# Seven block products for the output projection of a hybrid decoder step, with operand and weight sums woven in

## The chip, the cores and the metric

One Trainium2 chip, one core of it. The metric is the device time of one execution in microseconds, median of the runs. Engines: TensorE (PE for the matmuls, PEld for the loads of its stationary operand), VectorE (DVE), ScalarE (ACT), GpSimd (POOL) and SyncE (SP). Transfers are issued from two queues: SP's (`DMA`) and ACT's (`WDMA`, weights only).

## The reference

One layer of a decoder with three groups of heads (6 mLSTM "A", 6 gated DeltaNet "B", 4 HGRN2 "C", 128 wide each). 1024 prompt tokens, 16 meta tokens and 8 x 8 sample tokens pass through it, in float32:

```
h = rmsnorm(x) * norm_w
aq, ak, av, ao, ..., z = split(h @ w_in)          # w_in 2048 x 8984
hcat = concat(mlstm(...), gated_deltanet(...), hgrn2(...))   # 16 heads, chunked scans with state
y = headnorm(hcat) * out_norm_w * silu(z)         # tokens x 2048
x + y @ w_out                                     # w_out 2048 x 2048
y_prompt, y_sample = rmsnorm(x + y @ w_out) * final_norm_w
```

Besides the two y outputs the new states of all heads are returned. The change concerns the product `y @ w_out` for the 1024 prompt tokens.

## The kernel before, in words

The prompt is worked on in two halves of 512 tokens (`Half`); the first half carries the 64 sample tokens and the meta tokens as well. For each half, the input projection runs head by head in the order `ORDER` (C0 B0 A0 B1 A1 C1 B2 A2 B3 A3 C2 B4 A4 B5 A5 C3), and the heads' scans are interleaved with the matmuls of later heads. Then comes the output product for both halves.

Matmul precision: every float32 operand is split into a rounded part (hi) and a rest (lo), both in the fp32r type, and a product is hi·hi + hi·lo + lo·hi: three matmuls (two for the samples, whose hi and lo stand side by side as 128 columns).

Weights come as *pieces*: 128 x 512 float32 tiles in the order of the list `pieces`. `feed_raw` issues a piece's load on ACT's queue into one of 5 `wraw` buffers; `feed_split` makes `whi` (a cast on ACT) and `wlo` (a subtraction on DVE); `feed_ahead` keeps splits up to three pieces and loads up to seven pieces ahead of the piece in use. `o_raw` loads pieces of `w_out`.

Order of work: matmuls are written out in a fixed order. Everything else is a generator (`Stream`) in one of the queues of `Weave` (scan, fin, post, bg). A planner clock (`Clock`) adds up estimated costs per engine. After every matmul group, `pump` runs the next segment of each queue whose due time on TensorE's clock has come. A generator sets when its next segment is due by `ck.last`. `drain` moves the planner's clock on until a stream is done. Loads may be moved ahead by the scheduling framework as soon as their buffer is free, except those marked `keep_in_program_order`.

- `prep_B` (queue bg) prepares the second half's normalized input during the first half, through three `px` buffers, into DRAM (`hb_dram`).
- `gdn_scan` is a DeltaNet head: products on TensorE, coefficients sent through DRAM to give `Bb`, 15 steps of substitution on DVE (`substitute`), then doubling of the blocks (`pz`, `pyy`), then the chain over chunks (`pr`, `pw`, `pu2`, `po2`).
- `finish` (queue fin) normalizes a head's output, transposes it through DRAM, multiplies by `zs`, splits it into hi (ACT) and lo (POOL) and stores both parts in `y_dram`.

The output product before: for the first half and then the second, for each group `cg` of 512 output columns, 5 (or 4) token tiles accumulate over 16 heads `k` in PSUM banks `oacc`. At the end of a group, x is loaded, added on DVE, squared on ACT and multiplied by `final_norm_w` on POOL; `final_norm` scales and stores. The two last units have two token tiles each, so that little is left behind the last matmul. `load_y` brings the first half's y into the buffers of the projection's input, and the second half's y during the first half's last group.

Of the kernel before, what the change touches and what calls it, by code (L numbers as in the profile page):

```python
# [6 lines left out]
F32 = mybir.dt.float32  # L7
# [179 lines left out]
OUT_UNITS = ([(cg, range(5)) for cg in range(4)], [(cg, range(4)) for cg in range(3)] + [(3, range(2)), (3, range(2, 4))])  # L187
# [3 lines left out]
def hybrid_step(ctx, tc, i, o):  # L191
# [27 lines left out]
    def bank(name):  # L219
        return ps.tile([P, 512], F32, tag="ps", name=name)  # L220
# [22 lines left out]
    def o_raw(k, cg):  # L243
        raw = wp.tile([P, 512], F32, tag="wraw", name="wraw", bufs=5)
        WDMA(raw, i["w_out"][0, P * k:P * (k + 1), 512 * cg:512 * (cg + 1)])
        return raw

# [95 lines left out]
    for units in OUT_UNITS:  # L343
        for cg, _ in units:
            for k in range(NK):
                pieces.append((o_raw, k, cg))
# [256 lines left out]
    y_dram = [dp.tile([NH, P, w], F32R, name=f"y{w}") for w in (2 * NSAMP + 2 * HALF, 2 * HALF)]  # L603
# [233 lines left out]

    def finish(half, head, outs, ssq, scale, zs):
# [30 lines left out]
        yield  # L869
        yhi, ylo = zs.bitcast(F32R), y.bitcast(F32R)  # L870
# [4 lines left out]
        d = y_dram[half.index][head].bitcast(F32)  # L875
        for part, t in enumerate((yhi, ylo)):
            t = t.bitcast(F32)
            at_ = 2 * NSAMP if half.first else 0
            DMA(d[:, at_ + HALF * part:at_ + HALF * (part + 1)], t[:, 0:HALF])
            if half.first:  # L880
                DMA(d[:, NSAMP * part:NSAMP * (part + 1)], t[:, HALF:WS])
# [90 lines left out]
    def mlstm_scan(half, h, kT, qT, vT, tho, zs, nm, em, st):  # L972
# [118 lines left out]
        weave.add("fin", finish(half, h, hxs, ssq, 0.25, zs))  # L1091
# [60 lines left out]
    def gdn_scan(half, h, ck_, cq, cv, zs, Gb, eG, bb, st):  # L1152
# [65 lines left out]
        ready = ck.t["T"] + 7.0  # L1218
# [99 lines left out]
        ck.last += 8.0  # L1318
# [76 lines left out]
        weave.add("fin", finish(half, HA + h, hxs, ssq, 1.0, zs))  # L1395
# [22 lines left out]
    def hgrn_scan(half, h, kT, lf, qT, vT, zs, st):  # L1418
# [152 lines left out]
        weave.add("fin", finish(half, HA + HB + h, hxs, ssq, 0.25, zs))  # L1571
# [91 lines left out]
    def load_y(half, g):  # L1663
        w = y_dram[half.index].shape[-1]
        yT[half.index][g] = [hp.tile([P, 2, w], F32R, tag=f"h{g}{part}", name=f"y{g}{part}") for part in (0, 1)]
        for q in range(4):
            DMA(yT[half.index][g][q // 2][:, q % 2].bitcast(F32), y_dram[half.index][4 * g + q].bitcast(F32))

    def y_block(half, k, n, part):

        at_ = HALF * part + P * n
        return yT[half.index][k // 4][k % 4 // 2][:, k % 2, at_:at_ + P]

    hB, yT = {}, [{}, {}]
    for half, groups in zip(halves, group_lists):
        if not half.first:
            weave.drain_queue("bg")
            hT = hB
        seen = set()
        for n, group in enumerate(groups):  # L1680
            fresh = []
            for name, _, _ in group:
                if name not in seen:
                    seen.add(name)
                    fresh.append(name)
            if half.first and n == 6:
                weave.add("bg", prep_B())
            after = None
            if n == len(groups) - 1:
                if half.first:  # L1690
                    weave.drain_queue("bg")
                    after = load_hB
                else:
                    after = lambda g: load_y(halves[0], g)
# [12 lines left out]

    ys_flat = o["y_sample"].rearrange("b t d -> (b t) d")
    tags = ["a", "b", "c", "d", "e", "f", "g", "h", "j", "a", "b", "c", "d", "e", "f", "g", "h", "j", "k", "u"]

    def final_norm(toks, some, res, ss, fr, late):
        for n in some:
            cnt = toks[n][1]
            V.tensor_reduce(fr[:cnt, n:n + 1], ss[:cnt, n], op=ALU.add, axis=AX.X)
            V.tensor_scalar(fr[:cnt, 8 + n:9 + n], fr[:cnt, n:n + 1], 1.0 / D, EPS, op0=ALU.mult, op1=ALU.add)
            G.tensor_tensor(fr[:cnt, 16 + n:17 + n], fr[:cnt, 8 + n:9 + n], halfneg[:cnt, 0:1], op=ALU.pow)
        yield
        for n in some:
            _, cnt, _, dst = toks[n]
            for cg in range(4):  # L1720
                t, r = res[n, cg], fr[:cnt, 16 + n:17 + n]
                if cg == 3 and late:
                    V.scalar_tensor_tensor(t[:cnt], t[:cnt], r, fnw[cg][:cnt], op0=ALU.mult, op1=ALU.mult)
                elif cg == 3 or late and cg == 2:
# [4 lines left out]
                yield  # L1729

# [12 lines left out]
    fnw = []  # L1743
    for half in halves:
        toks = []
        for n, (c0, cnt) in enumerate(half.tiles):
            if half.first and n == 0:
                toks.append((0, NSAMP, xs_flat, ys_flat))
            else:
                a = HALF * half.index + c0  # L1750
                toks.append((c0, P, i["x_prompt"][0, a:a + P], o["y_prompt"][0, a:a + P]))
        nt = len(toks)
        ss = sp.tile([P, 8, 4], F32, tag="oss", name="oss")
        fr = sp.tile([P, 24], F32, tag="fr", name="fr")
        res = {}
        for cg, some in OUT_UNITS[half.index]:
            ccols = slice(512 * cg, 512 * (cg + 1))
            accs = {n: bank("oacc") for n in some}
            for k in range(NK):
                whi, wlo = next_piece()  # L1760
                for n in some:
                    yh, yl = (y_block(half, k, n, part) for part in (0, 1))
                    both = toks[n][1] == NSAMP
                    T.matmul(accs[n], yh, whi, start=k == 0, stop=False)
                    T.matmul(accs[n], yh, wlo, start=False, stop=both and k == NK - 1)
                    if not both:
                        T.matmul(accs[n], yl, whi, start=False, stop=k == NK - 1)
                    if n == some[0]:
                        feed_ahead()
                    weave.pump()  # L1770
                if half.first and cg == 3 and k % 4 == 3:
                    if k == 3:
                        weave.drain_queue("scan")
                        weave.drain_queue("fin")
                    load_y(halves[1], k // 4)
            if half.first and cg == 0:
                weave.drain_queue("scan")
                weave.drain_queue("fin")
                fnw = [sp.tile([P, 512], F32, tag=f"s{t}", name="fnw", bufs=1) for t in ("7", "8", "9", "B")]
                for t, c in zip(fnw, range(4)):  # L1780
                    DMA(t, i["final_norm_w"][512 * c:512 * (c + 1)].rearrange("(x d) -> x d", x=1).partition_broadcast(P))
                weave.add("bg", norm_states())
            weave.drain_queue("post")
            late = not half.first and cg == 3 and some[-1] == nt - 1
            for n in some:
                _, cnt, xsrc, _ = toks[n]
                t = row(tags[(nt * cg + n) % len(tags)], "res")[:, 0:512]
                DMA(t[:cnt], xsrc[:, ccols])
                ck.begin()
                V.tensor_tensor(t[:cnt], t[:cnt], accs[n][:cnt], op=ALU.add)  # L1790
                scr = sp.tile([P, 512], F32, tag="px", name="oscr", bufs=3)
                if cnt == NSAMP:
                    S.copy(scr[:cnt], accs[n][cnt:2 * cnt])
                    V.tensor_tensor(t[:cnt], t[:cnt], scr[:cnt], op=ALU.add)
                S.activation(scr[:cnt], t[:cnt], AF.Square, accum_out=ss[:cnt, n, cg:cg + 1])
                if not late:
                    G.tensor_tensor(t[:cnt], t[:cnt], fnw[cg][:cnt], op=ALU.mult)
                res[n, cg] = t
            if cg == 3:
                weave.add("post", final_norm(toks, some, res, ss, fr, late))  # L1800
# [35 lines left out]
```

## Time and profile before

| | |
|---|---|
| median of 3 runs | 2501.23 us (2497.94 to 2503.61) |
| the profiled execution | 2499.9 us, of which the span is 2498.2 us |
| mean granted TensorE clock | 0.991 |
| projections | to about 2097 us |
| output product | 2097.2 to 2487.5 us |
| behind the last matmul | 10.7 us |
| moved by DMA | 350.81 MB, 140 GB/s on average |

Busy times are per engine, in us. Matmul records overlap, as matmuls are pipelined, so a matmul's price is taken from the distance between starts. Nearly all instructions carry line L137, that of the recording helper, so groups are told apart by the names of their tiles: `oacc<-whi,y` is a matmul of the output product, `wlo<-wraw,whi` the split of a piece of weights, `res<-res,oacc` the sum out of PSUM.

### The profile page before, as it was taken

What the parts mean: (1) busy time and instruction counts of PE and PEld (TensorE: products, weight loads), DVE (VectorE), ACT (ScalarE), POOL (GpSimd) and SP (SyncE); (2) the same over time, 40 slices, a digit from 0 to 9 for tenths busy, and PEclk for the clock granted to TensorE, in tenths of its full rate; (3) what the DMA queues carried; (4) which work ended last, traced back from release to release, by engine and by line L of the source; (5) the groups of instructions that cost most, each with busy time, mean ns of one, the idle gap of its engine ahead of it and who ended that gap; (6) DMA issues with size and microseconds to landing.
All of it is one profiled execution on the core that took longest, in us unless ns stands there. A gap on an engine that the chain in (4) does not pass through costs nothing.

```text
span 2498.2 us, 43685 instructions
## 1 busy us (share of the span) xinstructions
PE 2437.1 (98%) x16032; PEld 2181.1 (87%) x16032; DVE 1441.9 (58%) x3080; ACT 993.4 (40%) x2428; POOL 548.7 (22%) x743
## 2 busy tenths in 40 slices
PE   6999999999999999999999999999999999999998
PEld 5999999999999999998787888888888888888886
DVE  7765766766647656556854556554654646333435
ACT  5643444443435334343642343343533334222324
POOL 5331211421204212113320113110310102111201
PEclk9999999999999999999999999999999999999999
DMA  6445756766645445348445445454544559526735
GB/s 138 111 119 144 175 131 135 187 147 159 147 108 142 99 119 146 93 112 244 112 121 123 112 120 135 118 134 98 144 118 112 132 124 307 135 84 201 252 100 181
DMA packets 681043, 350.81 MB, mean 140 GB/s; under 512 B 260004, under 2 KB 622076, under 8 KB 680828
## 3 DMA queue, kind: packets, MB, share of 16 engines
q10 hardware_dynamic: 318528, 185.64, 29.4%
q1 hardware_dynamic: 362300, 162.37, 24.9%
q8 instruction: 126, 2.06, 0.3%
q14 instruction: 89, 0.73, 0.1%
HBM read 285.71 MB, written 62.19 MB: 139 GB/s over the span
## 4 chain that ended last, share of the span: by engine, by line
PE 77%; DVE 8%; DMA 6%; issue 3%; ACT 2%; POOL 2%; SPq 1%; ACTq 0%; DVEq 0%; POOLq 0%
PE acc L137 53%; PE oacc L137 13%; DVE wlo L137 2%; DMA wraw<-in_w_in_dram 2%; PE pa L137 1%; PE po L137 1%; SPq L1209 1%; PE pyy L137 1%; PE nd L137 1%; DMA Bb<-db 1%; ACT whi L137 1%; PE pu L137 1%; PE pz L137 1%; DVE Yc L137 1%; DVE Yt L137 1%
## 5 line engine op out<-in xcount | busy, mean ns | idle before, releaser
L137 DVE TENSOR_TENSOR wlo<-wraw,whi 128x512 fp32r<-128x512 f32 x720 | 540.2, 752 | 552.5 <-ACT whi L137 534.7
L137 PE MATMUL acc<-hA,whi 128*128 128x288 f32 (+1 forms) x4544 | 819.6, 302 | 5.3 <-DVE whi L137 5.1
L137 ACT CAST whi<-wraw 128x512 fp32r<-128x512 f32 x720 | 443.9, 618 | 934.9 <-PE acc L137 427.5
L137 PE MATMUL acc<-hB,whi 128*128 128x512 f32 x2272 | 725.3, 401 | 3.6 <-DMA hB<-hblo 3.1
L137 PEld LDWEIGHTS acc<-hA,whi 128*128 128x128 f32 x4544 | 676.1, 190 | 10.2 <-issue 6.5
L137 PE MATMUL acc<-hA,wlo 128*128 128x288 f32 x2240 | 488.5, 298 | 4.7 <-DVE wlo L137 4.7
L137 PEld LDWEIGHTS acc<-hB,whi 128*128 128x128 f32 x2272 | 415.4, 190 | 85.6 <-DMA hB<-hblo 3.9
L137 PE MATMUL acc<-hB,wlo 128*128 128x512 f32 x1120 | 441.6, 394 | 1.5 <-DVE wlo L137 1.5
L137 PEld LDWEIGHTS acc<-hA,wlo 128*128 128x128 f32 x2240 | 365.7, 189 | 6.3 <-DVE wlo L137 6.3
L137 PE MATMUL oacc<-whi,y 128*128 128x512 f32 x1088 | 343.2, 390 | 0.0
L137 PEld LDWEIGHTS acc<-hB,wlo 128*128 128x128 f32 x1120 | 212.1, 189 | 49.4 <-DVE wlo L137 3.4
L137 PEld LDWEIGHTS oacc<-whi,y 128*128 128x128 f32 x1088 | 204.3, 188 | 42.8 <-ACT whi L137 0.8
L137 PE MATMUL oacc<-wlo,y 128*128 128x512 f32 x576 | 224.6, 390 | 2.0 <-DVE wlo L137 2.0
L137 PEld LDWEIGHTS oacc<-wlo,y 128*128 128x128 f32 x576 | 108.2, 188 | 25.4 <-DVE wlo L137 3.3
L137 POOL TENSOR_TENSOR res<-res,fnw 128x512 f32<-128x512 f32 (+1 forms) x34 | 48.6, 1460 | 258.5 <-ACT oscr L137 258.5
L137 POOL TENSOR_TENSOR y<-y,zs 128x592 fp32r<-128x592 f32 (+1 forms) x32 | 46.1, 1441 | 153.2 <-ACT zs L137 138.9
L137 POOL TENSOR_TENSOR qd<-qT,emb 128x512 f32<-128x512 f32 x12 | 16.9, 1404 | 219.1 <-PE po L137 219.0
L137 DVE TENSOR_TENSOR Yt<-Yc,Bb 128x60 f32<-128x60 f32 (+8 forms) x180 | 36.5, 203 | 47.5 <-DMA Bb<-db 42.4
L137 POOL TENSOR_TENSOR hr<-hr,halfneg 128x4 f32<-128x4 f32 (+1 forms) x48 | 44.7, 931 | 70.3 <-DVE hr L137 69.3
L137 POOL TENSOR_TENSOR nrm<-nrm,halfneg 128x10 f32<-128x10 f32 x12 | 24.0, 1998 | 125.0 <-DVE nrm L137 125.0
L137 POOL TENSOR_TENSOR X<-Ex,hk 128x256 f32<-128x256 f32 (+1 forms) x40 | 39.7, 992 | 52.4 <-PE pa L137 40.7
L137 DVE TENSOR_TENSOR Sx<-Sx,lf 128x256 f32<-128x256 f32 (+2 forms) x60 | 35.3, 590 | 20.8 <-ACT Ex L137 18.9
(416 smaller groups left out, 2748.4 us busy)
## 6 DMA issues: line engine op xcount, KB each, us to landing
wraw<-in_w_in_dram ACTq DMA_DIRECT2D x564, 256.0 KB
wraw<-in_w_out_dram ACTq DMA_DIRECT2D x144, 256.0 KB
y<-y SPq DMA_DIRECT2D x16, 576.0 KB
px<-in_x_prompt_dram SPq DMA_DIRECT2D x32, 256.0 KB
yd<-y SPq DMA_DIRECT2D x128, 64.0 KB
out_dram<-sst SPq DMA_DIRECT2D x16, 512.0 KB
s<-yd SPq DMA_DIRECT2D x32, 256.0 KB
y<-zs SPq DMA_DIRECT2D x32, 256.0 KB
```

Of the source, the lines that this page charges most:

```text
L137: return f(out, *a, **k)
L1209: DMA(db[j], Ball[SUB * j:SUB * (j + 1), 0:C, SUB * j:SUB * (j + 1)])
```

## The change: seven products

Let A be y as a 2 x 2 block matrix: rows are the first and second 512 prompt tokens, columns the first eight heads of `ORDER` (`K1`) and the last eight (`K2`). B is `w_out`, its rows cut by the same heads, its columns into two halves of 1024 (column groups j and j + 2, j = 0, 1). The eight block products become seven:

- T1 = B12 - B11, T3 = B22 - B12, T2 = B22 - T1, T4 = B21 - T2
- S1 = A21 + A22, S2 = S1 - A11, S3 = A11 - A21, S4 = A12 - S2
- phase 1: A11·B11, phase 2: A12·B21, phase 3: S2·T2, phase 4: S4·B22, phase 5: S1·T1, phase 6: S3·T3, phase 7: A22·T4; the results are sums of these.

What is done where:

- **Weights' sums.** `combine_weights`, in a new queue "mix", starts when `prep_B` is done and is drained in the middle of phase 1. In 16 rounds it loads four 128 x 512 tiles of `w_out` on SP's queue (held in program order), makes T1 to T4 in place on POOL, and stores them in DRAM (`w_comb`); `c_raw` later loads them as pieces.
- **A's sums.** The second half's `finish` no longer splits: it stores y once, in `y_whole`. During a phase, `fill` makes the next phase's left operand, head by head, in 16 steps and 4 more of the phase after: loads from `y_whole` (held in order, three buffers each, issued two steps ahead), sums on DVE and POOL, and three steps behind the sum a cast on ACT and a subtraction on DVE into the buffers `yT`.
- **Samples** are multiplied in phases 1 to 4 with the same pieces; in phase 3 they need pieces of their own (`other`), so 32 pieces are used there for 16.
- **Results.** x is loaded and added on POOL during the phases (`x_rows`, `x_added`); at the end of each of the two groups of a phase, DVE adds the four banks to one or two of the running sums. The last units are one of four tiles and two of two tiles, of 8 heads each.
- **DeltaNet.** `ready` is 10 after the loads of `Bb` are issued where it was 7, and the pause between the substitution and the doubling is 11 where it was 8 (planner's us).

The diff, cut to its core:

```diff
-        self.queues = {"scan": [], "fin": [], "post": [], "bg": []}
+        self.queues = {"scan": [], "fin": [], "post": [], "bg": [], "mix": []}
...
+HEADS = [{"A": 0, "B": HA, "C": HA + HB}[name[0]] + int(name[1]) for name in ORDER[1:]]
+K1, K2 = HEADS[:NH // 2], HEADS[NH // 2:]
+LAST_UNITS = [(0, range(4)), (1, range(2)), (1, range(2, 4))]
...
+    def c_raw(name, j, kk):
+        raw = wp.tile([P, 512], F32, tag="wraw", name="wraw", bufs=5)
+        WDMA(raw, w_comb[name][NK // 2 * j + kk])
+        return raw
...
+        if not half.first:
+            DMA(y_whole[head], y[:, 0:HALF])
+            return
         yhi, ylo = zs.bitcast(F32R), y.bitcast(F32R)
...
-        ready = ck.t["T"] + 7.0
+        ready = ck.t["T"] + 10.0
...
         yield from substitute()
-        ck.last += 8.0
+        ck.last += 11.0
...
+    def combine_weights():
+        while not prep_stream.done:
+            yield
+        for j in range(2):
+            for kk in range(NK // 2):
+                b11, b12, b21 = (sp.tile([P, 512], F32, tag="px", name="px", bufs=3) for _ in range(3))
+                b22 = sp.tile([P, 512], F32, tag="pxs", name="pxs", bufs=1)
+                for t, heads, cg in ((b11, K1, j), (b12, K1, j + 2), (b22, K2, j + 2), (b21, K2, j)):
+                    tc.keep_in_program_order(DMA(t, i["w_out"][0, P * heads[kk]:P * (heads[kk] + 1), 512 * cg:512 * (cg + 1)]))
+                for dst, a, b in ((b11, b12, b11), (b12, b22, b12), (b22, b22, b11), (b21, b21, b22)):
+                    ck.last = ck.t["T"] + 7.0
+                    yield
+                    G.tensor_tensor(dst, a, b, op=ALU.subtract)
+                ck.last = ck.t["T"] + 20.0
+                yield
+                for n, t in (("T1", b11), ("T3", b12), ("T2", b22), ("T4", b21)):
+                    DMA(w_comb[n][NK // 2 * j + kk], t)
+                    ck.last = ck.t["T"] + 3.0
+                    yield
+                ck.last = ck.t["T"] + 12.0
+                yield
...
+    def phase(u, j, accs, tiles, own=None, other=None, each=()):
+        for kk in range(NK // 2):
+            whi, wlo = next_piece()
+            for n in tiles:
+                yh, yl = (y_block(u, kk, n, part) for part in (0, 1))
+                T.matmul(accs[n], yh, whi, start=kk == 0, stop=False)
+                T.matmul(accs[n], yh, wlo, start=False, stop=False)
+                T.matmul(accs[n], yl, whi, start=False, stop=kk == NK // 2 - 1)
...
+            for g in filling:
+                next(g, None)
+            for f in each:
+                f(NK // 2 * j + kk)
...
+    def fill(at_, u, loads, ops, again=None):
+        for kk in range(NK // 2 + 2):
+            if kk < NK // 2:
+                for x, heads in enumerate(loads):
+                    weave.drain(fins[1, heads[kk]])
+                    tc.keep_in_program_order(DMA(beside[x][(at_ + kk) % 3], y_whole[heads[kk]]))
+                if again:
+                    DMA(yT[u][kk // 2][:, kk % 2, 2 * NSAMP:].bitcast(F32), y_dram[again[kk], :, 2 * NSAMP:].bitcast(F32))
+            if 0 < kk < NK // 2 + 1:
...
+                for e, a, b, op in ops:
+                    e.tensor_tensor(srcs[0], srcs[a], srcs[b], op=op)
+                    ck.sync()
+            yield
+            if kk > 1:
+                hi, lo = parts(u, kk - 2)
+                src = beside[0][(at_ + kk - 2) % 3]
+                ck.begin()
+                S.copy(hi, src)
+                ck.sync()
+                V.tensor_tensor(lo, src, hi, op=ALU.subtract)
+            yield
...
+    fill_with(0, [K1, K2], [(V, 0, ("hi", 0), LESS), (V, 0, ("lo", 0), LESS), (G, 0, 1, PLUS)])
+    for j in range(2):
+        accs, sacc = banks(), bank("oacc")
+        phase(1, j, accs, halfn, own=(sacc, samples(1)), each=[x_rows(1, 0, t1)])
+        ck.begin()
+        for n in halfn:
+            V.tensor_tensor(res[n + 1, j], res[n + 1, j], accs[n], op=ALU.add)
+            squared(n + 1, j)
+        sample_add(j, sacc)
...
+    fill_with(1, [], [(G, ("hi", 1), ("lo", 1), PLUS), (G, 0, ("hi", 0), LESS), (G, 0, ("lo", 0), LESS)])
+    for j in range(2):
+        accs, sacc = banks(), bank("oacc")
+        phase(0, j, accs, halfn, other=(sacc, samples(0)))
+        ck.begin()
+        for n in halfn:
+            V.tensor_tensor(t1[j, n], t1[j, n], accs[n], op=ALU.add)
+        sample_add(j + 2, sacc)
...
+    fill_with(0, [K1, K2], [(G, 0, 1, PLUS)])
...
+    fill_with(1, [K1], [(V, ("hi", 1), 0, LESS), (G, 0, ("lo", 1), PLUS)], again=K1)
...
+    fill_with(0, [K2], [])
```

More of the change, by code (lines that the diff above doesn't have):

```diff
@@ L1090, in mlstm_scan @@
         G.tensor_copy(Cn, last)
-        weave.add("fin", finish(half, h, hxs, ssq, 0.25, zs))
+        add_finish(half, h, hxs, ssq, 0.25, zs)
         if not half.first:
@@ L1729, in final_norm @@
                 yield
+            free.extend(res.pop((n, cg)) for cg in order)
     def norm_states():
@@ L1741, in norm_states @@
         yield
[L1743 to L1788, printed above, removed]
-                ck.begin()
[L1790 to L1800, printed above, removed]
@@ new lines, in x_load, with squared, sample_add @@
+    def x_load(n, cg):
+        t = free.pop(0)
+        cnt, src, _ = toks[n]
+        DMA(t[:cnt], src[:, 512 * cg:512 * (cg + 1)])
+        return t
+    def squared(n, cg, late=False):
+        cnt = toks[n][0]
+        t = res[n, cg]
+        S.activation(oscr[:cnt], t[:cnt], AF.Square, accum_out=ss[:cnt, n, cg:cg + 1])
+        if not late:
+            G.tensor_tensor(t[:cnt], t[:cnt], fnw[cg % 2][:cnt], op=ALU.mult)
+    def sample_add(cg, acc, first=False):
+        t = res[0, cg][:NSAMP]
+        ck.begin()
+        if first:
+            V.tensor_copy(t, acc[:NSAMP])
+        else:
+            V.tensor_tensor(t, t, acc[:NSAMP], op=ALU.add)
+        S.copy(oscr[:NSAMP], acc[NSAMP:2 * NSAMP])
+        V.tensor_tensor(t, t, oscr[:NSAMP], op=ALU.add)
@@ new lines, in fill_with, with x_rows, f, x_added @@
+    def fill_with(*a, **kw):
+        filling.append(fill(NK // 2 * len(filling), *a, **kw))
+    def x_rows(n0, cg0, sums):
+        def f(step):
+            j, x = step // 8, step % 8
+            if 1 <= x < 5:
+                res[x - 1 + n0, j + cg0] = x_load(x - 1 + n0, j + cg0)
+            if 3 <= x < 7:
+                t = res[x - 3 + n0, j + cg0]
+                G.tensor_tensor(t, t, sums[j, x - 3], op=ALU.add)
+        return f
+    def x_added(dst, j, n0, cg0, start):
+        pend = []
+        def f(step):
+            if step > start + 1 and pend:
+                t, x = pend.pop(0)
+                G.tensor_tensor(t, t, x, op=ALU.add)
+                free.append(x)
+            n = step - start
+            if n in halfn:
+                pend.append((dst[j, n], x_load(n + n0, j + cg0)))
+        return f
@@ new lines, in hybrid_step @@
+    weave.add("post", sample_done(2, 3))
+    weave.add("post", final_norm([0], range(4)))
+    fill_with(1, [K1], [(V, ("hi", 1), 0, LESS), (G, 0, ("lo", 1), PLUS)], again=K1)
+    for j in range(2):
+        accs = banks()
+        phase(0, j, accs, halfn, each=[at_step(5, lambda: free.extend(beside[1])), x_added(q, 0, 5, 2, 9)])
+        ck.begin()
+        for n in halfn:
+            V.tensor_tensor(res[n + 1, j + 2], res[n + 1, j + 2], accs[n], op=ALU.add)
+            squared(n + 1, j + 2)
+        for n in halfn:
+            q[j, n] = free.pop(0)
+            V.tensor_tensor(q[j, n], t1[j, n], accs[n], op=ALU.add)
@@ new lines, in hybrid_step @@
+    weave.add("post", final_norm(range(1, 5), range(4)))
+    fill_with(0, [K2], [])
+    added = [x_added(q, 1, 5, 2, 6), x_added(t1, 0, 5, 0, 9)]
+    for j in range(2):
+        accs = banks()
+        phase(1, j, accs, halfn, each=added)
+        ck.begin()
+        for n in halfn:
+            t = res[n + 5, j + 2] = q[j, n]
+            V.tensor_tensor(t1[j, n], t1[j, n], accs[n], op=ALU.add)
+            V.tensor_tensor(t, t, accs[n], op=ALU.add)
+            squared(n + 5, j + 2)
+    for j, tiles in LAST_UNITS:
+        accs = banks(tiles)
+        phase(0, j, accs, tiles, each=[at_step(3, lambda: load_fnw(0)), x_added(t1, 1, 5, 0, 1)] if j == 0 else ())
+        weave.drain_queue("post")
+        late = tiles[-1] == NC - 1 and j == 1
+        ck.begin()
+        for n in tiles:
+            t = res[n + 5, j] = t1[j, n]
+            V.tensor_tensor(t, t, accs[n], op=ALU.add)
+            squared(n + 5, j, late)
+        if j == 1:
+            weave.add("post", final_norm([n + 5 for n in tiles], (2, 3, 0, 1), late))
```

183 lines of the change are left out of this document (148 added, 35 removed).

## The prediction

> **What bounds the kernel now.** I read the page first (busy shares, the chain that ended last), then busy time by stage, then the chain inside the output product, then single tiles, waits and a few instructions.
>
> ```profile
> span 2498.2 us, 43685 instructions
> PE 2437.1 (98%) x16032; PEld 2181.1 (87%) x16032; DVE 1441.9 (58%) x3080; ACT 993.4 (40%) x2428; POOL 548.7 (22%) x743
> PE 77%; DVE 8%; DMA 6%; issue 3%; ACT 2%; POOL 2%; SPq 1%; ACTq 0%; DVEq 0%; POOLq 0%
> ...
> 680.00:1090.00 410.00, 407.27 (x3424) 398.50 (x3423) 238.92 (x581) 157.44 (x430) 90.21 (x131) 1.00 0.47 117
> 1200.00:1890.00 690.00, 684.79 (x3791) 567.06 (x3790) 394.44 (x807) 276.14 (x639) 136.31 (x152) 1.00 0.50 123
> 2061.00:2123.00 62.00, 62.00 (x298) 52.26 (x297) 37.28 (x67) 28.57 (x56) 17.43 (x19) 1.00 0.95 307
> 2097.00:2487.00 390.00, 388.02 (x1767) 320.70 (x1766) 165.27 (x250) 127.66 (x252) 72.25 (x59) 1.00 0.55 168
> 2311.00:2373.00 62.00, 61.77 (x272) 50.49 (x271) 28.72 (x54) 21.35 (x42) 16.16 (x14) 1.00 0.76 252
> ```
>
> Columns of the stages: length, busy PE, PEld, DVE, ACT, POOL, granted clock, DMA share, GB/s. TensorE is busy 388 of the 390 us of the output product (2097 to 2487) at clock 1.00, and 685 of 690 in the second half's projections. So matmuls taken out of this stage come off the end, as long as nothing takes over. DVE (165 of 390) and POOL (72) have room there now. That room is what the change spends.
>
> ```profile
> 2158.26 149.21 PE oacc L137 x658
> ...
> 2337.25 5.83 DMA res<-in_x_prompt_dram
> ...
> L137 PE MATMUL oacc<-whi,y x1088: 387/389/529, 2097.4 to 2487.3; 128*128 128x512 f32 x182
> L137 PE MATMUL oacc<-wlo,y x576: 387/389/504, 2097.6 to 2487.1; 128*128 128x512 f32 x192
> L137 DVE TENSOR_TENSOR wlo<-wraw,whi x142: 673/693/1843, 2097.0 to 2483.6; 128x512 fp32r<-128x512 f32 x142
> L137 DVE TENSOR_TENSOR res<-res,oacc x36: 671/678/687, 2154.9 to 2487.8; 128x512 f32<-128x512 f32 x32, 64x512 f32<-64x512 f32 x4
> L137 POOL TENSOR_TENSOR res<-res,fnw x34: 1280/1304/2181, 2157.6 to 2466.4; 128x512 f32<-128x512 f32 x30, 64x512 f32<-64x512 f32 x4
> L137 DVE TENSOR_SCALAR res<-res,fr x25: 466/473/1510, 2315.8 to 2492.1; 128x512 f32<-128x512 f32 x22, 64x512 f32<-64x512 f32 x3
> ```
>
> The first two rows are of the chain (start, length), the others of tiles (ns: least, median, most). A matmul record lasts 389 ns, but they overlap: the chain has 658 in 149.21 us, **226.8 ns each**, the price of one more or less.
>
> **The change, part by part.**
>
> **1. Matmuls taken out.** Now: 8 prompt tiles x 4 column groups x 16 k x 3 products = 1536, and 4 x 16 x 2 = 128 for the samples; 1664, the 1088 + 576 above. After: seven products x 2 groups x 8 k x 4 tiles x 3 = 1344, and the same 128: 1472. 192 fewer x 0.2268 = **-43.5 us**, all on the path. Pieces of weights fall from 144 to 136; their splits lie beside matmuls, so nothing is counted for them.
>
> **2. Operand sums and splits in the output product.** Per phase `fill` does eight items. Added on DVE: 40 splits (lo) and 24 sums (16 in the first fill, 8 in the fourth); on POOL: 48 sums (8, 24, 8, 8, 0), 16 `x_rows` adds and 16 `x_added` adds, beside the 34 multiplications by the final norm's weight that are there now; on ACT 40 casts and 8 copies. The question is what they do to each other:
>
> ```profile
> 2086.22 1.29 POOL L137 TENSOR_TENSOR y<-y,zs 128x512 fp32r<-128x512 f32 x1 [17.26 <-ACT zs L137]
> ...
> 2086.70 1.36 DVE L137 TENSOR_TENSOR wlo<-wraw,whi 128x512 fp32r<-128x512 f32 x1 [1.21 <-ACT whi L137]
> ```
>
> The split that started 0.48 us into a POOL operation took 1.36 us instead of 0.69: it gave up 0.67 of the 0.81 us of overlap. The adds out of PSUM (res<-res,oacc) never passed 687 ns, POOL busy or not. So I count POOL operations and DVE operations with two SBUF inputs as sharing one resource, at 0.69 and 1.30 us:
>
> Phase 2: DVE 36, POOL 19: 24.8 + 24.7 = 49.5 us beside 224 matmuls, 50.8 us.
> Phase 3: DVE 32 splits of weights (its samples use other weights than its products) + 10, POOL 28 (22 sums, 6 multiplications): 29.0 + 36.4 = 65.4 beside 50.8: **14.6 over**.
> Phase 4: 24 and 18: 40.0 beside 50.8.
> Phase 5: 31 and 18: 44.8 beside 43.5: 1.3 over.
> Phase 6: 25 and 17, with 12 scalings of 0.47: 45.0 beside 43.5: 1.5 over.
> Phase 7: 26 and 14, with 6 scalings: 38.9 beside 43.5.
>
> Over in all: 17.4 us. Splits run three pieces ahead; in phase 3 two pieces go in 3.17 us, so about 5 us of it is covered: **+12.5 us**. Below, the term is 0 (POOL's backlog runs into phase 4, which has 11 us to spare, and the weights' splits go ahead of it); above, DVE and POOL never overlap at all (the second rival). I take the middle, as the pair above stands nearest.
>
> [...]
>
> **3. Loads in the output product.** The second half's y is stored once, unsplit (16 stores of 256 KB for 32), and read as 48 loads of 256 KB plus 8 of 512 KB in place of 16 of 512 KB. Phase 5 moves 11.5 MB and phase 6 12.6 MB (weights 4.2, y 6.3 and 2.1, x 1.0 and 2.1, results 0 and 4.2) in 43.5 us each: 265 and 289 GB/s. The stage from 2061 to 2123 carried 307 GB/s with TensorE busy all 62.00 us, so I count 0. A held load is issued two steps (5.4 us) ahead of use; one x load took 5.83 us. Three buffers per operand let the queue run further ahead, which covers this; uncovered it would be 0.4 us x 40 items = 16 us. Behind a held load on SP's queue stand x loads and result stores, which have four steps.
>
> **4. Weights' sums during the projections.** 16 rounds of 4 loads, 4 POOL subtractions and 4 stores, paced on the planner's clock at 4 x 7.4 + 20.4 + 4 x 3.4 + 12.4 = 76 us: 1216 us in all.
>
> ```profile
> L650 SPq DMA_DIRECT2D hblo<-xT x64: 302/502/2326, 287.6 to 674.5; - x64
> ...
> PE acc L137 <- DVE wlo L137: 2.5, 5, 0.9
> ...
> DVE Yt L137 <- DMA Bb<-db: 42.4, 12, 5.3
> ...
> PE pyy L137 <- DVE s L137: 3.5, 6, 0.9
> PE pz L137 <- DVE Yc L137: 3.4, 1, 3.4
> ...
> PE pz L137 <- DVE X L137: 2.4, 1, 2.4
> ...
> 1374.82 0.39 PE L137 MATMUL nd<-s,qd 128*128 128x129 f32 x2
> ...
> 1408.39 0.60 PE L137 MATMUL pck<-ident,Ck 128*128 128x128 f32 x4
> ```
>
> They begin once the second half's input is stored (674.5 us) and end near 1891, some 230 us before the place in phase 1 that waits for them. POOL gets 64 x 1.30 = 83 us (136 of 690 busy there now). DMA gets 33.6 MB over 1216 us, 28 GB/s on top of 117 to 123. SP's queue gets 128 issues; head scans' small loads stand behind up to four 256 KB loads. Each subtraction can hold one split for 0.67 us: 43 us of DVE time, between 680 and 1890, where TensorE waited 2.5 us for splits (the second row). Bounds: 0 to 43 us; I take **+2**, near that row. In the second half's `finish`, 16 POOL subtractions and 16 casts go: nothing, they lay beside matmuls.
>
> **5. DeltaNet's delays.** `ready` 7 to 10 and the pause after the substitution 8 to 11: 6 us later per head, 12 heads. Cover: between the last nd of an mLSTM scan (1374.8) and the next DeltaNet's first pck (1408.4) the scans' queue is empty for 33 us. Without it, 72 us. DVE waited 42.4 us for Bb (12 waits, 3.5 each), most of which goes; TensorE waited only 3.5 + 3.4 + 2.4 = 9.3 us down that chain. **0**, with -9 as its low end.
>
> **6. The last tiles.** As now, two tiles are left behind the last matmul; its 10.7 us (2487.5 to 2498.2) stay.
>
> Sum against the profiled execution (span 2498.2, 2499.9 us in all): 2499.9 - 43.5 + 12.5 + 2 = 2470.9. The median of the runs, 2501.23, lies 1.3 above it: **2472 us**.
>
> **The rivals.**
> *The shared resource does not show* (phase 3's backlog passes into phase 4): terms 2 and 5 at their low ends give 2460, down to 2450. For it: TensorE waits 2 us for splits in the whole stage now. Against: POOL has 59 instructions there now and will have over 110.
> *DVE and POOL become the bound, slower.* DVE in the output stage by rows: 200 x 0.69 + 80 PSUM adds x 0.68 + 27 scalings x 0.47 + some 26 for the last scan and small ones = 231 us; POOL 114 x 1.30 + 20 = 168 us. Strictly in turn, as fills that wait for each other across in-order queues would make them, that is 399 us, and the stage is 390 now: 2499.9 + 9 + 2 + 1.3 = 2512. It decides from 390, that is, if under 9 us of the two overlap. For it: DVE's order puts a fill's sums and splits ahead of weights' splits. Against: PSUM adds at 687 ns at most, so part overlaps.
> [...]
> *Weights' sums hold the scans up.* The gain left, 31 us, is gone at 1.9 us of TensorE per round of 16: 2501, no change. For it: POOL is in order and the sums wait for loads. Against: the 33 us gaps.
> *Loads bind phases 5 and 6.* At 252 GB/s (the stage from 2311) 24.1 MB take 95.6 us, not 87: +8.7, 2481.
>
> **How the numbers follow.** Forecast 0.48 (2462 to 2490), loads 0.08, hidden 0.20, slower by turns 0.15, scans held 0.09, of which 0.07 within 0.2%, about what a measurement here can tell from no change. Faster 0.48 + 0.08 + 0.20 = 0.76, same 0.07, slower 0.17. From 2448 to 2506 leaves out the turns case and a little of the hidden one.
>
> **What would show it.** 1472 oacc matmuls at 227 ns; TensorE waiting for wlo or whi in the third phase, about 12 us, and hardly elsewhere in the product; wlo's mean there well above 0.8 us; the last weights' sum near 1890 us and the product starting within 5 us of 2097. I am wrong if the product takes over 375 us, if TensorE waits for an operand (y) rather than for weights, or if the projections end late.

## The result and the profile after

| | before | after |
|---|---|---|
| median of 4 runs each, side by side | 2502.42 us (2497.94 to 2508.23) | 2542.23 us (2536.53 to 2548.31) |
| ratio, after to before | | 1.0158, 95% interval 1.0126 to 1.0191 |
| profiled execution, its span | 2499.9, 2498.2 us | 2548.31, 2546.6 us |
| output product starts | 2097.2 us | 2141.4 us |
| output product ends | 2487.5 us | 2535.7 us |
| behind the last matmul | 10.7 us | 10.9 us |

The change made the kernel 1.6% slower; 2472 us had been forecast. The profiled execution of the kernel after is the slowest of its four, 6 us above their median. In the profiled executions the 48 us are lost in two places of nearly equal size: the projections end 44 us later, and the output product, which has 192 matmuls fewer, takes 394.3 us instead of 390.3.

From the page of the kernel after, the span, the busy times and the shares of the chain that ended last:

```profile
span 2546.6 us, 43916 instructions
...
PE 2433.0 (96%) x15840; PEld 2161.1 (85%) x15840; DVE 1583.9 (62%) x3178; ACT 1014.1 (40%) x2460; POOL 743.0 (29%) x871
...
PE 37%; DVE 5%; POOL 3%; DMA 3%; issue 3%; ACT 1%; SPq 0%; ACTq 0%; DVEq 0%; POOLq 0%
```

POOL has 128 instructions more than before and 194 us more busy time, 1.52 us for each; alone such an instruction takes 1.30. DVE has 98 more and 142 us more, 1.45 us for each where 0.69 is the price alone. That is the first sign that instructions of both engines have become longer. The same by stage, the second half's projections and the whole product (length, PE, PEld, DVE, ACT, POOL, granted clock, DMA share, GB/s):

```profile
1200.00:1890.00 690.00, 672.74 (x3703) 549.61 (x3702) 406.59 (x803) 272.16 (x625) 168.92 (x175) 0.99 0.55 141
...
2141.00:2535.70 394.70, 363.45 (x1577) 293.69 (x1575) 271.64 (x349) 152.73 (x299) 194.84 (x138) 0.95 0.57 181
```

TensorE idles 17 of 690 us in the projections (5 before) and 31 of 395 in the product (2 before), and the clock in the product is 0.95. The tiles of the product, and what TensorE waited for (us in total, times, longest):

```profile
L137 PE MATMUL oacc<-whi,y x960: 387/389/796, 2141.4 to 2535.5; 128*128 128x512 f32 x192
...
L137 PE MATMUL oacc<-wlo,y x512: 387/389/796, 2141.6 to 2535.3; 128*128 128x512 f32 x171
L137 DVE TENSOR_TENSOR res<-res,oacc x50: 669/678/689, 2236.7 to 2535.9; 128x512 f32<-128x512 f32 x44, 64x512 f32<-64x512 f32 x6
```

```profile
PE acc L137 <- DVE wlo L137: 15.0, 13, 2.2
PE oacc L137 <- DVE wlo L137: 14.8, 13, 2.7
PE oacc L137 <- DVE res L137: 12.7, 2, 7.5
PE pyy L137 <- DVE s L137: 11.4, 6, 3.2
```

The matmuls are the 1472 counted, and groups that nothing disturbs run at the forecast price (112 in 25.39 us, 226.7 ns each). But over the whole run the waits for splits are 15.0 us in the projections (6.2 before) and 14.8 in the product (2.0), DeltaNet's doubling (`pyy`) waits 11.4 (3.5), and two waits for a PSUM bank, 12.7 us, are new. Not all of it lies where the weights' sums run: from 690 us on, the projections' waits are 11.5 us for splits (2.5 before) and 6.9 for `pyy` (3.1). Matmuls reach 796 ns: the 62 of the product above 600 ns all lie in stretches with a granted clock of 0.50. Added up from the trace's records of the granted clock, 44.4 us of the projections behind 690 us ran at half clock (17.1 before) and 37.5 us of the product (none before). Matmuls of the product that follow each other without idle time start 427 ns apart there (median) and 227 elsewhere, so about half of such a time is lost; taken as half, the loss is 13.7 and 18.8 us more than before. In the product this closes: 29 us more of idle time and 19 of clock are 48, and 394.3 is the old 390.3 less 43.5 with 47.5 added. In the projections 20 us of idle and 14 of clock account for 34 of the 44. Another 4 were there at 690 us, before the first of the weights' sums (709.8): the kernel after had issued 5184 matmuls by then, the one before 5215, and it issued its 5184th 3.9 us earlier. The other 6 are not placed.

By groups of matmuls the product loses 21.3 us in the second half of phase 2, 10.6 in phase 3, 0 in phase 4, 8.3 in phase 5, 8.2 in phase 6 and 2.2 in phase 7. The worst stretches and the phase 4 behind them, by windows:

```profile
2194.00:2262.00 68.00, 57.37 (x232) 45.64 (x230) 48.17 (x48) 20.34 (x44) 43.75 (x29) 0.90 0.48 144
2262.00:2316.00 54.00, 44.70 (x169) 34.95 (x169) 42.16 (x44) 23.96 (x47) 37.82 (x25) 0.87 0.48 147
2316.00:2372.00 56.00, 55.45 (x245) 45.79 (x245) 36.98 (x49) 20.97 (x35) 16.18 (x10) 1.00 0.63 199
```

In the second row the 44 instructions of DVE and the 25 of POOL are busy for 80 us, where 0.69 and 1.30 each would make 63; in the third, with POOL at 16 us, TensorE idles for 0.6 us. What happens inside the first two, on DVE's and then POOL's timeline (start, length, tile; in brackets the idle time and its releaser):

```profile
2230.57 1.42 DVE L137 TENSOR_TENSOR yb<-yb,y 128x512 f32<-128x512 f32 x2 [3.18 <-DMA yb<-yw]
...
2233.65 0.69 DVE L137 TENSOR_TENSOR yb<-yb,y 128x512 f32<-128x512 f32 x1 [1.66 <-DMA yb<-yw]
...
2236.67 3.06 DVE L137 TENSOR_TENSOR res<-res,oacc 128x512 f32<-128x512 f32 x5
2240.45 0.69 DVE L137 TENSOR_TENSOR wlo<-wraw,whi 128x512 fp32r<-128x512 f32 x1 [0.72 <-ACT whi L137]
2241.06 1.78 DVE L137 TENSOR_TENSOR yb<-yb,y 128x512 f32<-128x512 f32 x1
...
2246.16 1.77 DVE L137 TENSOR_TENSOR res<-res,oscr 64x512 f32<-64x512 f32 x1
2247.86 1.77 DVE L137 TENSOR_TENSOR wlo<-wraw,whi 128x512 fp32r<-128x512 f32 x1
2249.56 5.18 DVE L137 TENSOR_TENSOR y<-yb,y 128x512 fp32r<-128x512 f32 x3
...
2263.16 1.09 DVE L137 TENSOR_TENSOR y<-yb,y 128x512 fp32r<-128x512 f32 x1 [6.75 <-ACT y L137]
```

```profile
2249.05 1.73 POOL L137 TENSOR_TENSOR yb<-yb 128x512 f32<-128x512 f32 x1
2250.75 1.74 POOL L137 TENSOR_TENSOR yb<-yb,y 128x512 f32<-128x512 f32 x1
2252.45 1.74 POOL L137 TENSOR_TENSOR yb<-y 128x512 f32<-128x512 f32 x1
```

From 2241 us on the two engines run in lock-step: an operation starts on each every 1.7 us, and each engine takes that long for what takes 0.69 and 1.28 us alone. At 2263.16 DVE has stood still for 6.75 us for a cast on ACT, which itself waited 8.84 us for POOL's sum (ACT's timeline):

```profile
2262.51 0.62 ACT L137 CAST y<-yb 128x512 fp32r<-128x512 f32 x1 [8.84 <-POOL yb L137]
```

The weights' splits queue behind that on both engines, although their data are there (the piece cast on ACT at 2263.04 had landed by 2238.4). On TensorE's timeline stand the waits that come of it; the first is for the bank that DVE frees at 2236.67, behind sums that had waited for loads of y (3.18 and 1.66 us above):

```profile
2237.40 0.79 PE L137 MATMUL oacc<-whi,y 128*128 128x512 f32 x1 [7.55 <-DVE res L137]
...
2256.47 0.56 PE L137 MATMUL oacc<-wlo,y 128*128 128x512 f32 x1 [2.06 <-DVE wlo L137]
...
2263.70 0.80 PE L137 MATMUL oacc<-whi,y 128*128 128x512 f32 x1 [2.41 <-ACT whi L137]
```

### The profile page after: what moved, and what is told of

Read it like the earlier page. It is cut to its first block, busy times and chain, and to the rows that moved or that the text cites. A ratio compares the mean times of both kernels' runs of the same rounds, so it can differ in the third digit from the quotient of the medians.

```text
span 2546.6 us, 43916 instructions
## 1 busy us (share of the span) xinstructions
PE 2433.0 (96%) x15840; PEld 2161.1 (85%) x15840; DVE 1583.9 (62%) x3178; ACT 1014.1 (40%) x2460; POOL 743.0 (29%) x871
## 4 chain that ended last, share of the span: by engine, by line
PE 37%; DVE 5%; POOL 3%; DMA 3%; issue 3%; ACT 1%; SPq 0%; ACTq 0%; DVEq 0%; POOLq 0%
PE acc L137 25%; PE oacc L137 7%; DVE wlo L137 2%; DMA yb<-yw 1%; POOL yb L137 1%; POOL res L137 1%; PE pa L137 1%; ACT whi L137 1%; PE pyy L137 1%; DVE y L137 0%; PE pz L137 0%; PE nd L137 0%; POOL X L137 0%; PE po L137 0%; DVE Yc L137 0%
## 5 line engine op out<-in xcount | busy, mean ns | idle before, releaser
L137 DVE TENSOR_TENSOR wlo<-wraw,whi 128x512 fp32r<-128x512 f32 x712 | 560.6, 790 | 457.0 <-ACT whi L137 405.4
L137 ACT CAST whi<-wraw 128x512 fp32r<-128x512 f32 x712 | 438.3, 618 | 889.9 <-PE acc L137 473.1
L137 PE MATMUL acc<-hB,whi 128*128 128x512 f32 x2272 | 733.3, 403 | 6.2 <-DMA hB<-hblo 2.6
L137 PE MATMUL acc<-hB,wlo 128*128 128x512 f32 x1120 | 444.5, 397 | 10.3 <-DVE wlo L137 10.3
L137 PE MATMUL oacc<-whi,y 128*128 128x512 f32 x960 | 314.6, 402 | 16.4 <-DVE res L137 12.7
L137 PEld LDWEIGHTS oacc<-whi,y 128*128 128x128 f32 x960 | 186.8, 195 | 58.4 <-DVE res L137 13.6
L137 PE MATMUL oacc<-wlo,y 128*128 128x512 f32 x512 | 207.0, 404 | 14.9 <-DVE wlo L137 14.8
L137 PEld LDWEIGHTS oacc<-wlo,y 128*128 128x128 f32 x512 | 99.6, 195 | 41.4 <-DVE wlo L137 21.0
L137 DVE TENSOR_TENSOR y<-yb,y 128x512 fp32r<-128x512 f32 x40 | 43.8, 1098 | 33.7 <-ACT y L137 32.7
L137 ACT CAST y<-yb 128x512 fp32r<-128x512 f32 x40 | 24.8, 621 | 88.2 <-POOL yb L137 52.3
L137 POOL TENSOR_TENSOR X<-Ex,hk 128x256 f32<-128x256 f32 (+1 forms) x40 | 38.6, 964 | 62.6 <-PE pa L137 51.4
L137 POOL TENSOR_TENSOR yb<-yb,y 128x512 f32<-128x512 f32 x24 | 37.3, 1559 | 48.8 <-DVE yb L137 47.3
```

Of the source, the lines that this page charges most:

```text
L137: return f(out, *a, **k)
```

## The experiments

Ratios are to the kernel before, run on the same chip, with the 95% interval; "start" is the start of the output product in the profiled execution. The theory after the result was that the weights' sums on POOL cost the 44 us of the projections, and the operand sums on POOL most of the product's; its rivals were the DeltaNet delays, the added transfers, POOL's in-order queue (an operation behind a sum that waits for a load) and the loads of y.

**1. No weights' sums.** `combine_weights` is not started; phases that use T1 to T4 load as many pieces of `w_out`.

```diff
-        WDMA(raw, w_comb[name][NK // 2 * j + kk])
+        heads, cg = {"T1": (K1, j), "T2": (K2, j + 2), "T3": (K1, j + 2), "T4": (K2, j)}[name]
+        WDMA(raw, i["w_out"][0, P * heads[kk]:P * (heads[kk] + 1), 512 * cg:512 * (cg + 1)])
...
-                weave.add("mix", combine_weights())
```

> The weights' sums are left out: the pieces of T1 to T4 are loaded straight from w_out, so the same bytes reach TensorE but not the sums (this part of the computation is changed). The product in the changed kernel starts at 2141 us where it started at 2097. Theory A (the weights' sums, with their POOL subtractions and transfers, delay the projections): the product starts within 12 us of 2097 and the time falls to 2500 to 2515. Theory C (DeltaNet's longer pauses delay them): the start stays near 2135 to 2141 and the time near 2540. Either way the product itself stays near 394 us from first to last matmul.

Measured: 2506.06 us, ratio 1.0006 (0.9996 to 1.0016); start 2098.6 us, product 395.3 us. The product starts 1.4 us later than before and not 44, so nearly all the lateness of the projections goes with the weights' sums (38 us by the ratios); the product keeps its loss.

**2. and 3. The delays**, taken back in the kernel after, and put alone into the kernel before.

```diff
-        ready = ck.t["T"] + 10.0
+        ready = ck.t["T"] + 7.0
...
-        ck.last += 11.0
+        ck.last += 8.0
```

> The changed kernel with DeltaNet's two delays put back to 7 and 8. Theory A: no change or a little worse, 2535 to 2550, as DVE waits longer for Bb again. Theory C: the start of the product falls back by 20 us or more, time under 2522.

> The kernel before with DeltaNet's two delays alone (10 and 11). Theory A: within 5 us of before. Theory C: the product starts 20 to 40 us later than 2097 and the time is 2520 to 2540.

Measured: 2543.48 us, 1.0162 (1.0139 to 1.0185), start 2139.4 with the old delays; 2505.02 us, 0.9999 (0.9987 to 1.0011), start 2093.3 with the new ones in the kernel before. The delays cost nothing and bring nothing. DVE's wait for `Bb`, which I had thought would mostly go, stayed; first after, then the delays alone (42.4 before):

```profile
DVE Yt L137 <- DMA Bb<-db: 47.6, 12, 6.7
```

```profile
DVE Yt L137 <- DMA Bb<-db: 43.6, 12, 5.2
```

**4. The sums' transfers only.** The 64 subtractions go; the 128 loads and stores stay.

```diff
-                    G.tensor_tensor(dst, a, b, op=ALU.subtract)
```

> The changed kernel in which the 64 POOL subtractions of the weights' sums are left out and their loads and stores stay (what is multiplied by is then not the sums). If POOL's work is what delays the projections (it holds DVE's two-input operations and stands ahead of the scans' own POOL work): the product starts within 15 us of 2097, time 2500 to 2515. If the transfers are (33.6 MB and 128 issues on SP's queue): the start stays at 2125 or later, time above 2525.

Measured: 2506.72 us, 1.0011 (1.0001 to 1.002); start 2096.8. The 33.6 MB and SP's issues cost 0.05% beside experiment 1, less than the intervals are wide. So it is the 64 operations on POOL, and not their transfers.

**5. The weights' sums on DVE.**

```diff
-                    G.tensor_tensor(dst, a, b, op=ALU.subtract)
+                    V.tensor_tensor(dst, a, b, op=ALU.subtract)
```

> The changed kernel with the weights' subtractions on DVE in place of POOL. With them left out the product started at 2097, with them on POOL at 2141. Theory P1 (POOL's operations exclude DVE's two-input operations, 64 x 0.69 us of splits held back): on DVE they take 64 x 0.69 us of DVE's own time, much the same 44 us: start 2130 to 2145. Theory P2 (POOL stands in line behind a late load, and the scans' POOL work behind it): POOL is free, but now DVE waits for the loads, with the splits behind it: start 2110 to 2145. If DVE has room and loads are in time: start within 10 us of 2097, time near 2508.

Measured: 2511.08 us, 1.0033 (1.0019 to 1.0047); start 2098.7. The waits for these loads now stand in DVE's queue (11.4 us in 7 waits; 46.9 in 8 on POOL after), and the engine that feeds TensorE does the work, yet 31 us come back, and 64 operations on DVE cost 0.2% beside experiment 4. A quarter of the subtractions after, and the same quarter here (least, median, most in ns):

```profile
L137 POOL TENSOR_TENSOR px<-px x16: 1278/1294/1740, 709.8 to 2012.6; 128x512 f32<-128x512 f32 x16
```

```profile
L137 DVE TENSOR_TENSOR px<-px x16: 645/692/1908, 711.0 to 1969.8; 128x512 f32<-128x512 f32 x16
```

DVE's busy time is the telling number. The page of this kernel:

```profile
PE 2409.3 (96%) x15840; PEld 2145.4 (86%) x15840; DVE 1584.7 (63%) x3242; ACT 1012.4 (40%) x2460; POOL 653.8 (26%) x807
```

64 instructions more on DVE, and it is busy 1584.7 us, where it was 1583.9 without them (and 1536.6 in experiment 4, with no sums at all):

```profile
PE 2411.3 (96%) x15840; PEld 2149.7 (86%) x15840; DVE 1536.6 (61%) x3178; ACT 1014.3 (41%) x2460; POOL 654.5 (26%) x807
```

So with the sums on POOL, DVE's own instructions became longer by as much as the sums take on DVE: 47.3 and 48.1 us over experiment 4.

**6. The sums without their transfers**, on tiles set once; pieces are loaded as in experiment 1. This leaves the weights' sums out of the result.

```diff
-                b11, b12, b21 = (sp.tile([P, 512], F32, tag="px", name="px", bufs=3) for _ in range(3))
...
-                    tc.keep_in_program_order(DMA(t, i["w_out"][...]))
...
-                    DMA(w_comb[n][NK // 2 * j + kk], t)
...
+        for t in (b11, b12, b21, b22):
+            G.memset(t, 1.0)
```

> The changed kernel with the 64 POOL subtractions on tiles that are set once, with no loads and no stores for them (the weights of T1 to T4 come straight from w_out, so the sums are not what is multiplied by). P1 (POOL's occupation itself): the start of the product stays near 2141, time above 2530. P2 (POOL waiting for loads, 46.9 us in 8 waits in the changed kernel): the start falls to within 15 us of 2097, time under 2518.

Measured: 2552.05 us, 1.0199 (1.0167 to 1.0231); start 2139.7. It does not tell what it was meant to: with no loads to wait for, the sums did not keep their spacing but ran in a bunch, and the lateness arose there. The first 110 us by window, and the longest waits of TensorE and DVE:

```profile
690.00:800.00 110.00, 83.61 (x681) 80.78 (x680) 46.68 (x88) 22.97 (x60) 96.20 (x81) 0.86 0.29 69
```

```profile
PE pz L137 <- DVE s L137: 22.3, 1, 22.3
...
DVE t L137 <- POOL hr L137: 28.1, 10, 21.5
```

POOL is busy 96 of 110 us, and a step of a scan on POOL (`hr`) stands behind the sums. So POOL's queue too can hold TensorE up when the sums come all at once, which they do not in the kernel after; how much of the loss here is the queue and how much DVE's longer instructions was not separated.

**7. A longer wait ahead of the first sum** of a round: 20 planner's us instead of 7, and 7 instead of 20 ahead of the stores.

```diff
-                    ck.last = ck.t["T"] + 7.0
+                    ck.last = ck.t["T"] + (20.0 if dst is b11 else 7.0)
...
-                ck.last = ck.t["T"] + 20.0
+                ck.last = ck.t["T"] + 7.0
```

> The changed kernel with the first subtraction of a round 20 us after its loads in place of 7, and the stores 7 us after the last one in place of 20, so a round is as long. P2: POOL no longer waits for the loads, the start falls to 2097 to 2115, time 2500 to 2518. P1: no change, 2535 to 2548.

Measured: 2525.9 us, 1.009 (1.0063 to 1.0118); start 2121.8. Inconclusive: POOL's waits for these loads did not go (15 waits, 65.7 us; 8 and 46.9 after), so the edit did not take away what it was to take away. Of the 20 us by which the product starts earlier, some 12 are less time at half clock (20.5 us for 44.4).

**8. POOL as busy, but without reading SBUF.** Each subtraction is replaced by three fills of constants, 512, 512 and 256 wide, which wait for the same loads; the weights' sums are left out of the result.

```diff
-                    G.tensor_tensor(dst, a, b, op=ALU.subtract)
+                    for w in (512, 512, 256):
+                        nc.gpsimd.memset(dst[:, 0:w], 0.0)
+                    ck.run("G", G.cost("tensor_tensor", dst, {}))
```

> The changed kernel in which each weights' subtraction on POOL is replaced by three memsets of 512, 512 and 256 columns of the same tile (1.3 us by the 522 ns that a memset of 512 took), behind the same load and ahead of the same store; the sums are left out. POOL is occupied as long and waits for the loads as before, but reads nothing. Theory port (POOL's reads exclude DVE's two-input operations): the start of the product falls from 2141 to within 12 us of 2097, time 2500 to 2515. Theory queue (the scans' POOL work stands behind, and TensorE's fixed order behind that): start 2120 to 2141, time 2525 to 2545.

Measured: 2510.75 us, 1.003 (1.0015 to 1.0045); start 2104.1. This decides between POOL's queue and what the expectation calls the port, the guess that POOL's reads of SBUF hold DVE's operations up. The projections from 690 to 2090 us, first after, then this kernel, then experiment 4:

```profile
690.00:2090.00 1400.00, 1364.11 (x8832) 1189.51 (x8831) 818.82 (x1728) 531.41 (x1301) 347.17 (x387) 0.98 0.55 144
```

```profile
690.00:2090.00 1400.00, 1385.52 (x9037) 1210.98 (x9036) 801.19 (x1768) 544.90 (x1332) 339.60 (x522) 1.00 0.58 150
```

```profile
690.00:2090.00 1400.00, 1389.84 (x9042) 1216.80 (x9041) 793.10 (x1764) 545.86 (x1335) 262.80 (x330) 1.00 0.58 151
```

POOL is as busy as after (340 and 347 us) and waits as long for the loads (42.3 us in 10 waits; 46.9 in 8), but TensorE issues 205 matmuls more in the same time and DVE does 40 instructions more in 18 us less. Occupying POOL with fills costs 0.2% beside experiment 4; the subtractions in their place, which read two tiles of SBUF each, cost 1.3% more. On the page:

```profile
PE 2412.8 (96%) x15840; PEld 2147.6 (86%) x15840; DVE 1546.0 (62%) x3178; ACT 1014.8 (40%) x2460; POOL 729.2 (29%) x999
```

The same 3178 DVE instructions as after take 1546.0 us, not 1583.9. The traces show where: set against the median of the same instruction beside an idle POOL, the 80 DVE instructions that overlap one of the sums in the kernel after are longer by 43.8 us in all, and the 137 that overlap a fill here by 9.2. Only 12.2 of the 43.8 us are in splits of weights; most of the rest is in steps of the scans. The queue theory falls for the kernel after.

Experiments 4 and 5, without the weights' sums on POOL, agree with that (start 2096.8 and 2098.7 us). DVE's sums out of PSUM, with one input in SBUF, did not become longer: 669 to 689 ns in the row above, 30 of the 50 beside a POOL operation.

**9. The operand sums on DVE.** The 48 sums on POOL in four of the five fills go to DVE; the weights' sums stay on POOL.

```diff
-    fill_with(0, [K1, K2], [(V, 0, ("hi", 0), LESS), (V, 0, ("lo", 0), LESS), (G, 0, 1, PLUS)])
+    fill_with(0, [K1, K2], [(V, 0, ("hi", 0), LESS), (V, 0, ("lo", 0), LESS), (V, 0, 1, PLUS)])
...
```

> The changed kernel with all 48 POOL sums of the operands of the product on DVE. The product takes 394 us from first to last matmul now (7 x 47 to 51 would be 334 of matmuls plus 9 for the last scan: 47 us of stalls, 21 in the second half of phase 2, 10 and 8 in phases 3 and 5, 8 in phase 6). If POOL's sums (1.7 us each while DVE's splits take 1.8) are what DVE and ACT wait for: stalls under 25 us, product 350 to 370, time 2500 to 2525. If DVE's own load is the bound, stalls stay above 40 us and the time within 10 us of 2542. The start of the product stays at 2141.

Measured: 2519.83 us, 1.0068 (1.0042 to 1.0093); product 372.9 us. The product by window:

```profile
2128.40:2501.30 372.90, 351.45 (x1575) 284.47 (x1573) 269.65 (x397) 153.36 (x299) 133.35 (x90) 1.00 0.61 192
```

48 operations more on DVE (397 for 349), and DVE is busy 2 us less than after; the clock is 1.00. The stall in phase 2's second half fell from 21.3 us to 5.5; phase 3 has 10.8 (10.6 after). The product's start moved too, 13 us earlier, though nothing ahead of it was edited: the time at half clock there is 17.1 us for 44.4, and 13.7 of the difference of 27.3 us is lost time. So the 44 us of one profile hold some 13 that differ from run to run of the same projections; the ratios, which are over several runs, put the weights' sums at 38 us (after less experiment 1).

**10. All sums on DVE** (experiments 5 and 9 together).

> Both moves at once: the 64 weights' subtractions and the 48 operand sums all on DVE. If the two prices are apart (31 us in the projections, 22 in the product) they add up: 2542 - 53 = 2489, product from 2099 for 373 us; faster than before by 0.4 to 0.8%. If DVE, which now does all of it, takes over as the bound, the product is longer than 385 us and the time 2500 or more.

Measured: 2491.16 us (2486.06 to 2497.3), 0.9945 (0.9925 to 0.9965). This beats the kernel before. Experiment 5 gained 31 us on the kernel after and experiment 9 gained 23; both together 53, so they add.

```profile
2105.60:2479.20 373.60, 353.12 (x1575) 285.63 (x1573) 270.36 (x397) 153.00 (x299) 133.18 (x90) 0.99 0.62 191
```

**11. Splits earlier.** On experiment 10, the casts and splits of an operand stand one step behind its sum instead of three.

```diff
-            if kk > 1:
-                hi, lo = parts(u, kk - 2)
-                src = beside[0][(at_ + kk - 2) % 3]
+            if kk > 0:
+                hi, lo = parts(u, kk - 1)
+                src = beside[0][(at_ + kk - 1) % 3]
```

> As the one with all sums on DVE, and each operand's cast and split one step behind its sum in place of three, so that its buffer is free for the next held load two steps (5 to 6 us) earlier. If late loads (DVE waited 16.4 us for them in phases 2 and 3 with the fills on DVE) carry the stalls that are left: 5 to 15 us less than without, 2475 to 2485. If DVE's own work does: within 4 us of it.

Measured: 2488.47 us (2482.13 to 2492.66), 0.9935 (0.9913 to 0.9956); product 371.1. The fastest kernel here with the full result, though its interval overlaps that of experiment 10: the step between sum and split is not what binds. DVE's wait for the loads of y, which the edit was to shorten, stayed (`yb` from `yw`: 17.8 us, 18.4 in experiment 10), so what late loads cost is not settled by it.

**12. No operand sums at all**, on experiment 10: the fills load and split, without sums, so the products are of the blocks themselves.

```diff
-    fill_with(0, [K1, K2], [(V, 0, ("hi", 0), LESS), (V, 0, ("lo", 0), LESS), (V, 0, 1, PLUS)])
+    fill_with(0, [K1, K2], [])
...
```

> As the one with all sums on DVE, with the operand sums left out: loads, casts and splits stay (what is multiplied is then not the sums). If sums on DVE are what is left of the stalls in the product (about 25 us there): product under 352 us, time 2465 to 2475. If loads or the splits themselves carry them: product 360 us or more.

Measured: 2475.71 us, 0.9885 (0.9861 to 0.9909); product 358.8. The sums on DVE thus still cost 15 us of the product; on POOL they cost 35 (394.3 less 358.8). Over the product of before less 43.5, that is 346.8, 12 us are left. By groups the stalls behind phase 1 are 3.2 us in phase 2, 0.9 in phase 3, 2.0 in phase 5, 5.3 in phase 6 and 4.4 in phase 7, 15.8 in all, of which the product before had 3.6 as well. Splits of y, the adds of x on POOL and the loads and stores still stand there; DVE's splits of y wait 38.6 us for ACT's casts in the product of this kernel (25 waits). Which of them costs the 12 us was not tried.

## Why the prediction was wrong

*Matmuls taken out, -43.5 us: right.* 1472 remain, at 227 ns.

*Weights' sums, +2 us: the step that failed.* They cost 38 us by the ratios; in the profile the projections end 44 later. With the next term this is the whole miss: 36 and 35 us too little, where the result is 70 above the forecast. The prediction had the mechanism and the upper bound, 43 us, and then chose +2 because TensorE waited only 2.5 us for splits in that stage of the kernel before. That wait row says how much slack is used, not how much is left: nothing in it shows that 0.67 us can be added in front of a split. And it was a row of splits alone: of the 43.8 us by which DVE's instructions beside the sums became longer, 12.2 are in splits, the rest mostly in the scans' steps, which TensorE waits for as well. The rival "weights' sums hold the scans up" named the right place, with a price of 1.9 us per round from which the gain is gone; the price was 2.4 (38 us) to 2.75 (44 us). Its reason, sums that wait for loads in POOL's queue, was the wrong one (experiment 8). Had the upper bound been taken, this term would have been right within 5 us and the forecast 2513.

*Sums and splits in the product, +12.5 us: right mechanism, wrong size.* It was 47.5. Of that, 35 are the operand sums, of which 21 go when they move to DVE. The price of a pair was not too low: 0.69 and 1.30 us had been counted one after the other, 1.99, and in lock-step a pair took 1.7. What failed is adding up each phase's busy time, as if all its work could be done in any order. That missed order: a cast on ACT waits for POOL's sum (8.84 us above), DVE's split waits for that cast (6.75), and weights' splits and the emptying of a bank stand behind, so 7.55 and 5.2 us were lost for banks, which no term had. And it missed the clock: 18.8 us. The forecast put the loss into phase 3; the second half of phase 2 was worst. How the 35 us divide between lock-step and order was not tried apart.

*"DVE and POOL become the bound", 2512 us: nearer, and short too.* It took the product to 399 us with the two strictly in turn. The product took 394, but not because the two fill it: DVE was busy 272 and POOL 195 of 395 us, and phase 4 lost nothing.

*Loads, 0: not shown.* TensorE's waits were for splits and banks, but the 7.55 us for a bank stand behind two waits of DVE for loads of y, 10.3 us of which it had in the product. Without any sums all that is left is 12 us, loads included.

*DeltaNet's delays, 0: right* (experiments 2 and 3), but not for the reason given: the wait for `Bb` did not shrink. *The last tiles, 0: right*, 10.9 for 10.7.

*Signs named beforehand.* Some 12 us of waits for splits were named for phase 3 and hardly any elsewhere; TensorE waited for `wlo` for 1.5 us there and 14.8 in the whole product, so that these two numbers lie close is luck. The last of the weights' sums ran at 2017 us, not near 1890. The two signs of being wrong, a product over 375 us and projections that end late, both came.

Even with all sums on DVE the kernel is 19 us over the forecast: 14 in the product (373.6 for 359.3) and the start 8 us later than before (2 forecast). Of those 8, 6 were there at 690 us, before the first sum (5167 matmuls issued by then, 5215 before); experiment 5 started at 2098.7 with the same sums. What the 6 come from is open.

## What to carry to other kernels

Before work goes to POOL because it looks idle, ask whether it reads SBUF beside DVE operations that do so too: here 112 sums moved from POOL to the busier DVE turned 1.6% slower into 0.6% faster, and fills that read nothing, in place of the 64 weights' sums, left 0.3% of the 1.6. A term for a shared resource in a stage where TensorE has no idle time should be taken at its upper bound, as a small wait before (2.5 us here) does not say how much the wait can grow. Read an engine's busy time against its instruction count in two kernels: more time for the same instructions (38 us here) was time lost inside them, which the lists of waits did not show.

## What the hardware showed that was not expected

- Two engines in lock-step: an operation of DVE and one of POOL each took 1.7 us when they alternated on two-input sums (2241 to 2256 us), where one alone takes 0.69 and 1.30.
- Half clock behind short waits. Behind the wait of 2.06 us that ended at 2256.47 stands a stretch of 3.41 us at half clock, and at the end of one of 2.41 a stretch of 6.8:

```profile
2256.77:2260.18 3.41, 3.41 (x9) 2.65 (x8) 0.00 (x0) 0.00 (x0) 3.41 (x4) 0.50 0.27 77
...
2263.60:2270.40 6.80, 5.22 (x11) 3.76 (x12) 4.70 (x4) 1.77 (x5) 6.57 (x5) 0.50 0.14 39
```

In the first of them matmuls start 0.43 us apart where 0.23 is usual, so nearly half of it is lost, and that wait of 2 us cost nearly 4. It is no rule: behind a wait of 2.92 us that ended at 1206.81 the clock stayed at 1.00, and in the kernel before such a stretch stands at 1615.64 behind a wait of 0.46. Up to the last matmul the stretches at half clock in the kernel after are 3.41, 6.83, 10.24 or 13.65 us long. What sets the clock back was not worked out.
